# Gates and gated products of two mixers computed with tokens on the partitions, with the gated sum transposed

## The chip, the cores and the metric

The kernel runs on one core of one Trainium2 chip. The metric is the device time of one launch in microseconds (us); the comparison is by medians of several runs. The engines are named PE (TensorE, matrix multiplications), DVE (VectorE), ACT (ScalarE), POOL (GpSimd) and SP (SyncE, which here only starts the weight transfers). PSUM is the memory into which PE adds up its results; DVE and ACT read it.

## The reference

The input x has 256 tokens of 1024 features, in float32. Two blocks follow one another. In outline (the attention branches themselves are cut):

```python
# first block
h    = rmsnorm(x, norm_mix)
proj = h @ w_in                      # queries, keys, values, ..., and 2 x 1024 gate columns
o_a  = dsa_mixer(...)                # 256 x 512
o_b  = nsa_mixer(...)                # 256 x 512
mix  = (sigmoid(gate_a) * (o_a @ w_branch_a)
        + sigmoid(gate_b) * (o_b @ w_branch_b))
x    = x + mix @ w_out
x    = x + square(relu(rmsnorm(x) @ w_mlp_in)) @ w_mlp_out
# second block: swiglu, hybrid mixer, swiglu; the mixer ends with
merged = (sigmoid(g_a) * (att @ w_att_branch)       # att: 256 x 512
          + sigmoid(g_m) * (ml @ w_mlstm_branch))   # ml: 256 x 1024
y      = merged @ w_out
```

The change is in the four sigmoid gates, the four products that they multiply, and the two sums `mix` and `merged`.

## The kernel before

**Precision by splitting.** Every float32 operand of a large product is split in two parts, `hi` (rounded) and `lo` (the rest), and a product is three matmuls: hi·hi, hi·lo and lo·hi. Weights come in units of 512 KB (2 tiles of 128 rows by 512 columns) on SP's queue, five units ahead (`stream_dma`); `stream_split` makes `hi` on ACT (L262) and `lo` on DVE (L263), two units ahead.

**Two forms of a product.** One chunk is 512 columns of a weight matrix with K rows.
- `gemm_feat` (L335 to L360) keeps 128 columns of the weights in PE (the stationary operand) and moves all 256 tokens past them (L349, L351, L352). For K = 1024 a chunk is 8 x 4 x 3 = 96 matmuls of 256 columns. The result has features on the partitions.
- `gemm_tok` (L285 to L330) keeps 128 tokens in PE and moves 512 weight columns past them (L305, L306, L307). The same chunk is 8 x 2 x 3 = 48 matmuls of 512 columns. The result has tokens on the partitions, in two tiles, `t` = 0 and 1. With `tail=n` the last n units go to token tile 0 first and then to tile 1, so that tile 0 is complete earlier.

Each of the two forms fills two PSUM buffers of 128 x 512 per chunk; the pool `pacc` has three. A function `done` empties each as it is complete.

**Pending jobs.** Other work (attention steps, transposes) waits in a list, `pending`. Both forms take `rate` jobs from it after each tile of K, from tile `delay` on, so this work lies between the matmuls of a chunk. What is written between them is then moved again: the program's scheduler sets the order on PE, ACT and DVE by its own estimate of times; POOL and SP follow the order as written.

**From tokens to features.** A product needs its left operand with features on the partitions. `split_T` makes such an operand from a token tile by jobs; for each tile of K, `split_one` runs two PE transposes (L399), one ACT copy that makes `hi` (L406) and one DVE subtraction that makes `lo` (L407). Where the data has features on the partitions already, `split_sb` does it without PE (L1124 on ACT, L1125 on DVE).

**First mixer.** Chunks 5 to 8 of `W_IN1` are the gates (L1008). Each half chunk is multiplied on DVE by the inverse norm of its tokens (`bc2`, L1002), passes through Tanh on ACT (L1003) and is scaled on POOL (L1004). Between these matmuls the attention steps are taken from the list: logits (L869), row maximum and bias on DVE (L882), exp on ACT (L887), transposes (L896), copies to SBUF on DVE (L898), products with the values (L909). Then come `W_BRB` and `W_BRA` (K = 512, two chunks each): `bdone` (L1025) multiplies by the gate, `adone` (L1032, L1033) does the same, adds and calls `split_sb`. `W_OUT1` follows with `gemm_tok`.

**Second mixer.** Chunks 18 to 21 of `W_IN2` are the gates `gta` and `gtm` (L1542, L1543), among the chunks of a convolution (`cdone`) that keeps features on the partitions. The output gate `gto` of chunks 16 and 17 is done by tokens already: one Tanh that reads PSUM with a scale per token (L1493). `W_ATT` (K = 512) and `W_MLB` (K = 1024) are the gated products, and the sum `mb` goes through `split_sb` to `W_OUT2`, which is in `down_post`.

The three functions of the diff are the first mixer, `down_post` and the second mixer.

Of the kernel before, what the change touches and what calls it, by code (L numbers as in the profile page):

```python
# [9 lines left out]
F32 = mybir.dt.float32  # L10
# [3 lines left out]
AF = mybir.ActivationFunctionType  # L14
ALU = mybir.AluOpType
# [6 lines left out]
D = 1024  # L22
# [187 lines left out]
class Prog:  # L210
# [352 lines left out]
    def block1_mix(self, x0, x):  # L563
        tc, nc, ap, g = self.tc, self.nc, self.ap, self.g
        with ExitStack() as es, ExitStack() as rs_:
# [431 lines left out]
            gate = cp.tile([128, 16, 256], F32, name="gate")  # L997

            def gdone(c):
                def f(i, ps):  # L1000
                    gsl = gate[:, 4 * c + 2 * i:4 * c + 2 * i + 2, :]
                    nc.vector.tensor_tensor(gsl, ps, bc2, op=ALU.mult)  # L1002
                    nc.scalar.activation(gsl, gsl, AF.Tanh, scale=0.5)  # L1003
                    nc.gpsimd.tensor_scalar(gsl, gsl, 0.5, 0.5, op0=ALU.mult, op1=ALU.add)  # L1004
                return f
            for c in range(4):
                self.gemm_feat(W_IN1, 5 + c, *xT, gdone(c))
                if c == 0:  # L1008
                    bias_rows(0)
# [7 lines left out]
            mixt = self.xp.tile([128, 8, 256], F32, tag="x", name="mixt")  # L1017
            mTp = rpool("mixT", 1)
            l3p = rpool("late", 2)
            mT = [mTp.tile([128, 8, 256], F32R, name="mT%d" % i) for i in range(2)]  # L1020

            def bdone(c):
                def f(i, ps):
                    k = 4 * c + 2 * i
                    nc.vector.tensor_tensor(mixt[:, k:k + 2, :], ps, gate[:, 8 + k:10 + k, :], op=ALU.mult)  # L1025
                return f

            def adone(c):
                def f(i, ps):
                    k = 4 * c + 2 * i  # L1030
                    ma = l3p.tile([128, 2, 256], F32, tag="ma", name="ma")
                    nc.vector.tensor_tensor(ma, ps, gate[:, k:k + 2, :], op=ALU.mult)  # L1032
                    nc.vector.tensor_tensor(ma, ma, mixt[:, k:k + 2, :], op=ALU.add)  # L1033
                    self.split_sb(ma, mT, k)
                return f
            self.later(*ja)
            for c in range(2):
                self.gemm_feat(W_BRB, c, *obT, bdone(c))
                self.gemm_feat(W_BRA, c, *oaT, adone(c))
# [3 lines left out]
            def odone(c):  # L1043
                def f(t, ps):
                    cs = slice(c * 512, c * 512 + 512)
                    nc.vector.tensor_tensor(x[:, t, cs], ps, x[:, t, cs], op=ALU.add)
                return f
            for c in range(2):
                self.gemm_tok(W_OUT1, c, *mT, odone(c), delay=1, rate=2)
                self.later(*jx[4 * c:4 * c + 4])  # L1050
# [100 lines left out]
    def down_post(self, W, hT, gi, x, mul, name, rs=None, gcol=None):  # L1151
# [61 lines left out]
        self.gemm_tok(W, 0, *hT, done0, delay=1, rate=2)  # L1213
# [34 lines left out]
    def mixer2(self, x):  # L1248
        tc, nc, ap, g = self.tc, self.nc, self.ap, self.g
        xT, js = self.nextT  # L1250
        with ExitStack() as es, ExitStack() as rs_:
# [283 lines left out]
            gta = g2p.tile([128, 8, 256], F32, name="gta")  # L1535
            gtm = g2p.tile([128, 8, 256], F32, name="gtm")
            bc2 = rsB.unsqueeze(1).to_broadcast([128, 2, 256])

            def gfeat(dst, c):
                def f(i, ps):  # L1540
                    gsl = dst[:, 4 * c + 2 * i:4 * c + 2 * i + 2, :]
                    nc.vector.tensor_tensor(gsl, ps, bc2, op=ALU.mult)  # L1542
                    nc.scalar.activation(gsl, gsl, AF.Tanh, scale=0.5)  # L1543
                    nc.gpsimd.tensor_scalar(gsl, gsl, 0.5, 0.5, op0=ALU.mult, op1=ALU.add)
                return f
# [5 lines left out]
            self.gemm_feat(W_IN2, 18, *xT, gfeat(gta, 0))  # L1551
            self.gemm_feat(W_IN2, 12, *xT, cdone(2))
            self.gemm_feat(W_IN2, 19, *xT, gfeat(gta, 1))
# [49 lines left out]
            self.gemm_feat(W_IN2, 20, *xT, gfeat(gtm, 0))  # L1603
            self.later(job(mpv, 2), job(mpv, 3), job(mnorm, 2))
            self.gemm_feat(W_IN2, 21, *xT, gfeat(gtm, 1))
            self.flush()

            mgt = self.xp.tile([128, 8, 256], F32, tag="x", name="mgt")

            def adone(c):  # L1610
                def f(i, ps):
                    fs = slice(4 * c + 2 * i, 4 * c + 2 * i + 2)
                    nc.vector.tensor_tensor(mgt[:, fs, :], ps, gta[:, fs, :], op=ALU.mult)
                return f

            def mdone(c):
                def f(i, ps):
                    k = 4 * c + 2 * i
                    fs = slice(k, k + 2)
                    mb = m4p.tile([128, 2, 256], F32, tag="mb", name="mb")  # L1620
                    nc.vector.tensor_tensor(mb, ps, gtm[:, fs, :], op=ALU.mult)
                    nc.vector.tensor_tensor(mb, mb, mgt[:, fs, :], op=ALU.add)
                    self.split_sb(mb, mT, k)
# [30 lines left out]
```

## Time and profile before

| | us |
|---|---|
| median of 3 runs (lowest, highest) | 1115.84 (1114.71, 1116.51) |
| the profiled execution, its own time | 1113.66 |
| its span in the profile | 1111.9 |
| PE busy (6852 matmuls) | 1094.0 |
| PE weight loads busy | 978.1 |
| DVE busy | 760.2 |
| ACT busy | 574.0 |
| POOL busy | 95.9 |

The span is the time from the first to the last instruction in the profile; 1.8 us of the execution's own time lie around it. The granted clock of TensorE was its higher level all through the span. A matmul's record goes from its start to the modelled end of its results, so the records of neighbouring matmuls overlap, and the distance between the starts of two is what one of them takes of PE's time. The products of the change lie between 75 and 186 us (first mixer) and between 749 and 891 us (second mixer).

### The profile page before, as it was taken

The page shows a single profiled execution, that of the slowest core. Times are in us where ns is not written, and L with a number is a line of the kernel's source. Part 1 is how long each engine was busy: PE and PEld are TensorE (multiplying, and loading weights), DVE is VectorE, ACT ScalarE, POOL GpSimd, SP SyncE. Part 2 cuts the span into 40 slices and gives each one's busy share as a digit, 9 for nine tenths or more (in the row PEclk, how much of TensorE's full clock was granted, in tenths as well). Part 3 has the DMA queues.
Part 4 walks back from the last instruction along what each step waited for, and adds up shares of the span by engine and source line. Part 5 has one row for each costly group of instructions (what it writes and reads, how often), then busy time and mean ns, then how long its engine had stood idle before and what let it go on. Part 6 is the DMA issues. An engine that isn't in the chain of part 4 may idle for free.

```text
span 1111.9 us, 17700 instructions
## 1 busy us (share of the span) xinstructions
PE 1094.0 (98%) x6852; PEld 978.1 (88%) x6852; DVE 760.2 (68%) x1230; ACT 574.0 (52%) x858; POOL 95.9 (9%) x143
## 2 busy tenths in 40 slices
PE   8999999999999999999999999999999999999997
PEld 8898899888888788888879999889999978888886
DVE  6777768587745487776457675557788776777643
ACT  6334554465545365555545336455466456655552
POOL 0422410000001000000010100001313000000000
PEclk9999999999999999999999999999999999999999
DMA  8864235565555556555556646434545465555552
GB/s 298 238 231 114 77 111 182 182 190 190 190 193 191 192 180 191 190 190 190 190 159 202 206 137 209 150 120 162 173 152 172 159 199 165 182 185 189 189 177 89
DMA packets 56036, 196.91 MB, mean 177 GB/s; under 512 B 6844, under 2 KB 7116, under 8 KB 55696
## 3 DMA queue, kind: packets, MB, share of 16 engines
q1 hardware_dynamic: 52704, 186.44, 51.6%
q0 software_dynamic: 2960, 9.21, 3.4%
q8 instruction: 54, 0.88, 0.3%
q14 instruction: 30, 0.25, 0.1%
q10 hardware_dynamic: 288, 0.14, 0.1%
HBM read 192.84 MB, written 1.44 MB: 175 GB/s over the span
## 4 chain that ended last, share of the span: by engine, by line
PE 93%; DMA 3%; DVE 2%; ACT 1%; issue 0%; POOL 0%; DVEq 0%; SPq 0%; ACTq 0%; POOLq 0%
PE acc L368 20%; PE acc L369 10%; PE acc L305 10%; PE acc L306 10%; PE acc L307 10%; PE acc L349 8%; PE acc L351 8%; PE acc L352 8%; PE o L909 1%; PE sm L869 1%; DMA w1k<-in_cmp_w_k 1%; PE tr L896 1%; PE o L1455 1%; PE sm L1425 1%; PE tr L399 1%; DMA w1v<-in_cmp_w_v 1%
## 5 line engine op out<-in xcount | busy, mean ns | idle before, releaser
L263 DVE TENSOR_TENSOR lo<-raw,hi 128x1024 fp32r<-128x1024 f32 (+2 forms) x356 | 431.7, 1215 | 255.0 <-ACT hi L262 253.0
L262 ACT ACTIVATE hi<-raw 128x1024 fp32r<-128x1024 f32 (+2 forms) x356 | 371.2, 1044 | 422.2 <-PE acc L351 128.9
L368 PE MATMUL acc<-xs,hi 128*128 128x512 f32 x960 | 338.5, 398 | 1.3 <-DVE sum L374 1.0
L369 PE MATMUL acc<-xs,lo 128*128 128x256 f32 x960 | 267.6, 280 | 0.0
L368 PEld LDWEIGHTS acc<-xs,hi 128*128 128x128 f32 x960 | 180.7, 189 | 43.8 <-DVE sum L374 1.4
L349 PE MATMUL acc<-xs,hi 128*128 128x256 f32 (+1 forms) x696 | 198.1, 287 | 0.3 <-ACT hi L262 0.3
L351 PE MATMUL acc<-xs,hi 128*128 128x256 f32 (+1 forms) x696 | 197.7, 285 | 0.0
L352 PE MATMUL acc<-xs,lo 128*128 128x256 f32 (+1 forms) x696 | 196.9, 285 | 0.1
L369 PEld LDWEIGHTS acc<-xs,lo 128*128 128x128 f32 x960 | 181.6, 189 | 0.5
L349 PEld LDWEIGHTS acc<-xs,hi 128*128 128x128 f32 (+1 forms) x696 | 132.4, 191 | 3.1 <-issue 1.9
L351 PEld LDWEIGHTS acc<-xs,hi 128*128 128x128 f32 (+1 forms) x696 | 132.9, 191 | 1.9 <-issue 1.3
L352 PEld LDWEIGHTS acc<-xs,lo 128*128 128x128 f32 (+1 forms) x696 | 132.4, 191 | 1.5 <-issue 1.0
L305 PE MATMUL acc<-hi,hT 128*128 128x512 f32 x304 | 117.9, 390 | 1.0 <-DVE x L1087 1.0
L306 PE MATMUL acc<-lo,hT 128*128 128x512 f32 x304 | 118.5, 390 | 0.0
L307 PE MATMUL acc<-hi,hT 128*128 128x512 f32 x304 | 118.0, 389 | 0.0
L305 PEld LDWEIGHTS acc<-hi,hT 128*128 128x128 f32 x304 | 57.0, 188 | 13.3 <-DVE x L1087 1.5
L307 PEld LDWEIGHTS acc<-hi,hT 128*128 128x128 f32 x304 | 57.1, 188 | 12.0
L306 PEld LDWEIGHTS acc<-lo,hT 128*128 128x128 f32 x304 | 57.1, 188 | 11.6
L305 PE MATMUL acc<-hi,xs 128*128 128x386 f32 (+1 forms) x128 | 47.7, 375 | 1.6 <-DVE f L1178 1.5
L306 PE MATMUL acc<-lo,xs 128*128 128x386 f32 (+1 forms) x128 | 47.9, 375 | 0.0
L307 PE MATMUL acc<-hi,xs 128*128 128x386 f32 (+1 forms) x128 | 46.7, 370 | 0.0
L374 DVE TENSOR_TENSOR sum<-acc,sum 128x512 f32<-128x512 f32 x60 | 41.0, 684 | 0.0
(430 smaller groups left out, 1333.0 us busy)
## 6 DMA issues: line engine op xcount, KB each, us to landing
raw<-in_w_in SPq DMA_DIRECT2D x100, 512.0 KB, 3.7
raw<-in_ffn_w_gate SPq DMA_DIRECT2D x44, 512.0 KB, 4.2
raw<-in_ffn_w_up SPq DMA_DIRECT2D x44, 512.0 KB, 4.3
raw<-in_ffn_w_down SPq DMA_DIRECT2D x44, 512.0 KB, 4.2
raw<-in_w_mlp_in SPq DMA_DIRECT2D x32, 512.0 KB, 3.3
raw<-in_w_mlp_out SPq DMA_DIRECT2D x32, 512.0 KB, 3.3
raw<-in_w_out SPq DMA_DIRECT2D x16, 512.0 KB, 3.6
raw<-in_w_in SPq DMA_DIRECT2D x16, 386.0 KB, 3.1
```

What stands on the lines that cost most here:

```text
L262: nc.scalar.activation(hi[:, :n * w], raw[:, :n * w], AF.Copy)
L263: nc.vector.tensor_tensor(lo[:, :n * w], raw[:, :n * w], hi[:, :n * w], op=ALU.subtract)
L305: nc.tensor.matmul(ps[t][:, :w], xh[:, k, sl], hi, start=(k == 0), stop=False)
L306: nc.tensor.matmul(ps[t][:, :w], xh[:, k, sl], lo, start=False, stop=False)
L307: self.last_mm = nc.tensor.matmul(ps[t][:, :w], xl[:, k, sl], hi, start=False, stop=last)
L349: nc.tensor.matmul(o, hi[:, fs], xh[:, k, :], start=(k == 0 and f % 2 == 0), stop=False, skip_group_check=True)
L351: nc.tensor.matmul(o, hi[:, fs], xl[:, k, :], start=False, stop=False, skip_group_check=True)
L352: nc.tensor.matmul(o, lo[:, fs], xh[:, k, :], start=False, stop=last, skip_group_check=True)
L368: nc.tensor.matmul(ps[:, f, :, :], hi[:, fs], x.both[:, k, :, :], start=(k == 0), stop=False)
L369: nc.tensor.matmul(ps[:, f, 0, :], lo[:, fs], x.hi[:, k, :], start=False, stop=last)
L374: nc.vector.tensor_tensor(s, ps[:, :, 0, :], s, op=ALU.add)
L399: nc.tensor.transpose(ps[:, i * 128:i * 128 + 128], src(t, k), self.ident)
```

## The change

In both mixers the gate chunks and the gated products go from `gemm_feat` to `gemm_tok`. The gate tiles and the sums have tokens on the partitions. The multiplication by the inverse norm is left out as an instruction of its own: it becomes the per-token scale of a Tanh that reads PSUM (in the first mixer a small DVE instruction makes the scale `rh0`). The sum is written back to `mixt` and `mgt`, and eight `split_T` jobs in each mixer (`jm`, sixteen PE transposes) take the place of four calls of `split_sb`. The second chunk of `W_BRA` and of `W_MLB` completes token tile 0 first (`tail`), and the products after them start to take jobs one tile of K later (`delay=2`).

```diff
-            gate = cp.tile([128, 16, 256], F32, name="gate")
+            gate = cp.tile([128, 2, 2 * D], F32, name="gate")
+            rh0 = self.small(2, "r0h")
+            nc.vector.tensor_scalar(rh0, r0, 0.5, None, op0=ALU.mult)
 
             def gdone(c):
-                def f(i, ps):
-                    gsl = gate[:, 4 * c + 2 * i:4 * c + 2 * i + 2, :]
-                    nc.vector.tensor_tensor(gsl, ps, bc2, op=ALU.mult)
-                    nc.scalar.activation(gsl, gsl, AF.Tanh, scale=0.5)
+                def f(t, ps):
+                    gsl = gate[:, t, c * 512:c * 512 + 512]
+                    nc.scalar.activation(gsl, ps, AF.Tanh, scale=rh0[:, t:t + 1])
                     nc.gpsimd.tensor_scalar(gsl, gsl, 0.5, 0.5, op0=ALU.mult, op1=ALU.add)
                 return f
             for c in range(4):
-                self.gemm_feat(W_IN1, 5 + c, *xT, gdone(c))
+                self.gemm_tok(W_IN1, 5 + c, *xT, gdone(c))
...
-            mixt = self.xp.tile([128, 8, 256], F32, tag="x", name="mixt")
+            mixt = self.xp.tile([128, 2, D], F32, tag="x", name="mixt")
...
+            jm = self.split_T(lambda t, k: mixt[:, t, k * 128:k * 128 + 128], range(8), [0, 1], *mT)
...
             def adone(c):
-                def f(i, ps):
-                    k = 4 * c + 2 * i
-                    ma = l3p.tile([128, 2, 256], F32, tag="ma", name="ma")
-                    nc.vector.tensor_tensor(ma, ps, gate[:, k:k + 2, :], op=ALU.mult)
-                    nc.vector.tensor_tensor(ma, ma, mixt[:, k:k + 2, :], op=ALU.add)
-                    self.split_sb(ma, mT, k)
+                def f(t, ps):
+                    cs = slice(c * 512, c * 512 + 512)
+                    ma = l3p.tile([128, 512], F32, tag="ma", name="ma")
+                    nc.vector.tensor_tensor(ma, ps, gate[:, t, cs], op=ALU.mult)
+                    nc.vector.tensor_tensor(mixt[:, t, cs], ma, mixt[:, t, cs], op=ALU.add)
                 return f
             self.later(*ja)
             for c in range(2):
-                self.gemm_feat(W_BRB, c, *obT, bdone(c))
-                self.gemm_feat(W_BRA, c, *oaT, adone(c))
+                self.gemm_tok(W_BRB, c, *obT, bdone(c))
+                self.gemm_tok(W_BRA, c, *oaT, adone(c), tail=c)
+                self.later(*jm[4 * c:4 * c + 4])
...
             for c in range(2):
-                self.gemm_tok(W_OUT1, c, *mT, odone(c), delay=1, rate=2)
+                self.gemm_tok(W_OUT1, c, *mT, odone(c), delay=1 if c else 2, rate=2)
                 self.later(*jx[4 * c:4 * c + 4])
...
-        self.gemm_tok(W, 0, *hT, done0, delay=1, rate=2)
+        self.gemm_tok(W, 0, *hT, done0, delay=2 if self.pop else 1, rate=2)
...
             self.gemm_feat(W_IN2, 10, *xT, cdone(0))
-            self.gemm_feat(W_IN2, 18, *xT, gfeat(gta, 0))
+            self.gemm_tok(W_IN2, 18, *xT, gdone(gta, 0))
             self.gemm_feat(W_IN2, 12, *xT, cdone(2))
-            self.gemm_feat(W_IN2, 19, *xT, gfeat(gta, 1))
+            self.gemm_tok(W_IN2, 19, *xT, gdone(gta, 1))
...
-            self.gemm_feat(W_ATT, 0, *attT, adone(0))
-            self.gemm_feat(W_ATT, 1, *attT, adone(1), rate=2)
+            self.gemm_tok(W_ATT, 0, *attT, adone(0))
+            self.gemm_tok(W_ATT, 1, *attT, adone(1), rate=2)
...
+            jm = self.split_T(lambda t, k: mgt[:, t, k * 128:k * 128 + 128], range(8), [0, 1], *mT)
             for c in range(2):
-                self.gemm_feat(W_MLB, c, *mlT, mdone(c), delay=1)
+                self.gemm_tok(W_MLB, c, *mlT, mdone(c), delay=1, tail=2 * c)
+                self.later(*jm[4 * c:4 * c + 4])
```

The left-out parts do for `bdone`, the second mixer's `adone`, `mdone` and the chunks 20 and 21 what the parts shown do.

The end of the first mixer's attention on PE, before. `L869` are logits, `L909` products with the values, `L896` transposes of the softmax; `xs` and `hi` or `lo` in `acc<-xs,hi` are the tokens and the weights of a gate chunk.

```order
L349 MATMUL acc<-xs,hi 128x256
L869 MATMUL sm<-ka,qa 128x128 x6
L909 MATMUL o<-tms,PT 128x64 x8
L869 MATMUL sm<-ka,qa 128x128
L896 MATMUL tr<-ident,L 128x128 x8
L351 MATMUL acc<-xs,hi 128x256
L352 MATMUL acc<-xs,lo 128x256
L349 MATMUL acc<-xs,hi 128x256
```

These are the last logits; 121 gate matmuls follow them, among the rest of the attention, up to the first matmul of `W_BRB`. Now the same place after the change; the last gate matmul stands five rows above the first row, and `ob` and `obT` are the attention's output and its transposed form.

```order
L896 MATMUL tr<-ident,L 128x128 x5
L869 MATMUL sm<-ka,qa 128x128 x8
L909 MATMUL o<-tms,PT 128x64 x4
L896 MATMUL tr<-ident,L 128x128 x4
L909 MATMUL o<-tms,PT 128x64 x4
L896 MATMUL tr<-ident,L 128x128 x4
L399 MATMUL tr<-ident,ob_1079 128x128
L399 MATMUL tr<-ident,ob_1080 128x128
L909 MATMUL o<-tms,PT 128x64 x4
L305 MATMUL acc<-hi,obT_1076 128x512
L306 MATMUL acc<-lo,obT_1076 128x512
```

The gate matmuls have moved ahead of the last logits, and between the last steps of the attention there are a few matmuls of `W_BRB`, of which the first two rows are shown.

The start of `W_OUT1` on PE, before: `oaT` is the left operand of `W_BRA`, `mT` that of `W_OUT1`.

```order
L351 MATMUL acc<-oaT_1075,hi 128x256
L352 MATMUL acc<-oaT_1074,lo 128x256
L305 MATMUL acc<-hi,mT_2156 128x512
L306 MATMUL acc<-lo,mT_2156 128x512
L307 MATMUL acc<-hi,mT_2157 128x512
```

`W_OUT1` ran through its tiles of K without a break. After the change, from the last matmuls of its first four tiles of K on:

```order
L305 MATMUL acc<-hi,mT_1958 128x512
L306 MATMUL acc<-lo,mT_1958 128x512
L307 MATMUL acc<-hi,mT_1959 128x512 x2
L399 MATMUL sm<-ident,mixt 128x128
L399 MATMUL tr<-ident,mixt 128x128
L399 MATMUL sm<-ident,mixt 128x128
L399 MATMUL tr<-ident,mixt 128x128
L305 MATMUL acc<-hi,mT_1958 128x512
L399 MATMUL sm<-ident,mixt 128x128
L399 MATMUL tr<-ident,mixt 128x128
```

Of the 16 new transposes of the first mixer eight stand here, behind the first 24 matmuls of `W_OUT1`. The single `L305` between them belongs to the second chunk of `W_OUT1`.

## Rows read from the trace of the kernel before

**Rows 1.** The page: busy time of each engine, and the chain's shares by engine.

```profile
PE 1094.0 (98%) x6852; PEld 978.1 (88%) x6852; DVE 760.2 (68%) x1230; ACT 574.0 (52%) x858; POOL 95.9 (9%) x143
...
PE 93%; DMA 3%; DVE 2%; ACT 1%; issue 0%; POOL 0%; DVEq 0%; SPq 0%; ACTq 0%; POOLq 0%
```

**Rows 2.** Windows: stretch, length, busy PE, PEld, DVE, ACT, POOL (instructions), clock, DMA, GB/s.

```profile
75.00:150.00 75.00, 75.00 (x612) 67.83 (x611) 55.06 (x179) 40.01 (x126) 20.77 (x24) 1.00 0.35 99
...
625.00:650.00 25.00, 25.00 (x211) 25.00 (x210) 17.01 (x19) 8.47 (x8) 2.51 (x6) 1.00 0.58 171
830.00:854.00 24.00, 23.95 (x190) 23.36 (x188) 21.71 (x34) 12.52 (x18) 9.28 (x10) 1.00 0.51 159
1050.00:1075.00 25.00, 25.00 (x112) 20.71 (x111) 12.05 (x11) 9.98 (x10) 0.00 (x0) 1.00 0.60 193
```

**Rows 3.** Costliest groups, one of each form: instructions, busy us, mean ns.

```profile
L349 PE MATMUL acc<-xs,hi 128*128 128x256 f32 (+1 forms) x696 | 198.1, 287 | 0.3 <-ACT hi L262 0.3
...
L305 PE MATMUL acc<-hi,hT 128*128 128x512 f32 x304 | 117.9, 390 | 1.0 <-DVE x L1087 1.0
```

**Rows 4.** Timeline of PE, `gemm_feat`: start, duration; first and last of 43 matmuls.

```profile
624.90 0.28 PE L349 MATMUL acc<-xs,hi 128*128 128x256 f32 x1
...
629.94 0.28 PE L349 MATMUL acc<-xs,hi 128*128 128x256 f32 x1
```

**Rows 5.** Timeline of PE, `gemm_tok`: the first and the last of 46 matmuls.

```profile
1055.78 0.39 PE L307 MATMUL acc<-hi,hT 128*128 128x512 f32 x1
...
1065.98 0.39 PE L307 MATMUL acc<-hi,hT 128*128 128x512 f32 x1
```

**Rows 6.** Timeline of PE, four transposes between matmuls of `gemm_tok`.

```profile
202.02 0.40 PE L307 MATMUL acc<-hi,mT 128*128 128x512 f32 x1
202.25 0.38 PE L399 MATMUL sm<-ident,x 128*128 128x128 f32 x2
202.47 0.38 PE L399 MATMUL tr<-ident,x 128*128 128x128 f32 x2
202.61 0.49 PE L305 MATMUL acc<-hi,mT 128*128 128x512 f32 x1
202.93 0.39 PE L306 MATMUL acc<-lo,mT 128*128 128x512 f32 x1
```

**Rows 7.** Timeline of PE, two logits matmuls between gate matmuls.

```profile
88.70 0.28 PE L351 MATMUL acc<-xs,hi 128*128 128x256 f32 x1
88.91 0.70 PE L869 MATMUL sm<-kv,qb 64*128 64x256 f32 x2
89.53 0.39 PE L352 MATMUL acc<-xs,lo 128*128 128x256 f32 x1
89.76 0.28 PE L349 MATMUL acc<-xs,hi 128*128 128x256 f32 x1
```

**Rows 8.** Groups by line and form: instructions, busy us, mean ns, idle before them.

```profile
L263 DVE TENSOR_TENSOR lo<-raw,hi 128x1024 fp32r<-128x1024 f32 x332 | 409.6, 1236 | 243.0 <-ACT hi L262 241.1 <-PE sm L399 0.6
...
L898 DVE COPY PT<-tr 128x512 f32<-128x512 f32 x18 | 12.0, 684 | 5.0 <-PE tr L896 5.0
...
L887 ACT ACTIVATE L<-L,nn 128x128 f32<-128x128 f32 x24 | 9.3, 389 | 5.1 <-DVE nn L885 5.0
L887 ACT ACTIVATION_READ_ACCUMULATOR L<-L,nn 128x1 f32 x48 | 9.0, 187 | 0.0
...
L1002 DVE TENSOR_TENSOR gate<-acc,rsB 128x512 f32<-128x512 f32 x8 | 5.5, 689 | 2.1 <-PE acc L352 2.0
...
L399 PE MATMUL tr<-ident,x 128*128 128x128 f32 x28 | 5.2, 274 | 0.5 <-DVE x L1046 0.5
...
L1493 ACT ACTIVATE gto<-acc,m_rh 128x512 f32<-128x512 f32 x4 | 2.7, 689 | 2.6 <-PE acc L307 2.6
...
L407 DVE TENSOR_TENSOR obT<-tr,obT 128x256 fp32r<-128x256 f32 x4 | 1.7, 420 | 0.0
...
L406 ACT ACTIVATE obT<-tr 128x256 fp32r<-128x256 f32 x4 | 1.5, 378 | 3.5 <-PE tr L399 3.4
```

More of the change, by code (lines that the diff above doesn't have):

```diff
@@ L1020, in block1_mix, with f @@
             mT = [mTp.tile([128, 8, 256], F32R, name="mT%d" % i) for i in range(2)]
+            jm = self.split_T(lambda t, k: mixt[:, t, k * 128:k * 128 + 128], range(8), [0, 1], *mT)
             def bdone(c):
-                def f(i, ps):
-                    k = 4 * c + 2 * i
-                    nc.vector.tensor_tensor(mixt[:, k:k + 2, :], ps, gate[:, 8 + k:10 + k, :], op=ALU.mult)
+                def f(t, ps):
+                    cs = slice(c * 512, c * 512 + 512)
+                    nc.vector.tensor_tensor(mixt[:, t, cs], ps, gate[:, t, D + c * 512:D + c * 512 + 512],
+                                            op=ALU.mult)
                 return f
             def adone(c):
-                def f(i, ps):
-                    k = 4 * c + 2 * i
-                    ma = l3p.tile([128, 2, 256], F32, tag="ma", name="ma")
-                    nc.vector.tensor_tensor(ma, ps, gate[:, k:k + 2, :], op=ALU.mult)
-                    nc.vector.tensor_tensor(ma, ma, mixt[:, k:k + 2, :], op=ALU.add)
-                    self.split_sb(ma, mT, k)
+                def f(t, ps):
+                    cs = slice(c * 512, c * 512 + 512)
+                    ma = l3p.tile([128, 512], F32, tag="ma", name="ma")
+                    nc.vector.tensor_tensor(ma, ps, gate[:, t, cs], op=ALU.mult)
+                    nc.vector.tensor_tensor(mixt[:, t, cs], ma, mixt[:, t, cs], op=ALU.add)
                 return f
@@ L1534, in mixer2 @@
             wp = rpool2("mw", 2)
[L1535 to L1545, printed above, removed]
+            gta = g2p.tile([128, 2, D], F32, name="gta")
+            gtm = g2p.tile([128, 2, D], F32, name="gtm")
             hm = hp.tile([128, 2, 4, 256], F32, name="hm")
@@ L1602, in mixer2, with f @@
             self.later(*jh[0:4], job(mst, 2), job(mst, 3))
-            self.gemm_feat(W_IN2, 20, *xT, gfeat(gtm, 0))
+            self.gemm_tok(W_IN2, 20, *xT, gdone(gtm, 0))
             self.later(job(mpv, 2), job(mpv, 3), job(mnorm, 2))
-            self.gemm_feat(W_IN2, 21, *xT, gfeat(gtm, 1))
+            self.gemm_tok(W_IN2, 21, *xT, gdone(gtm, 1))
             self.flush()
-            mgt = self.xp.tile([128, 8, 256], F32, tag="x", name="mgt")
+            mgt = self.xp.tile([128, 2, D], F32, tag="x", name="mgt")
             def adone(c):
-                def f(i, ps):
-                    fs = slice(4 * c + 2 * i, 4 * c + 2 * i + 2)
-                    nc.vector.tensor_tensor(mgt[:, fs, :], ps, gta[:, fs, :], op=ALU.mult)
+                def f(t, ps):
+                    cs = slice(c * 512, c * 512 + 512)
+                    nc.vector.tensor_tensor(mgt[:, t, cs], ps, gta[:, t, cs], op=ALU.mult)
                 return f
             def mdone(c):
[L1617 to L1623, printed above, removed]
+                def f(t, ps):
+                    cs = slice(c * 512, c * 512 + 512)
+                    mb = m4p.tile([128, 512], F32, tag="mb", name="mb")
+                    nc.vector.tensor_tensor(mb, ps, gtm[:, t, cs], op=ALU.mult)
+                    nc.vector.tensor_tensor(mgt[:, t, cs], mb, mgt[:, t, cs], op=ALU.add)
                 return f
             self.later(None, *jh[4:8])
-            self.gemm_feat(W_ATT, 0, *attT, adone(0))
-            self.gemm_feat(W_ATT, 1, *attT, adone(1), rate=2)
+            self.gemm_tok(W_ATT, 0, *attT, adone(0))
+            self.gemm_tok(W_ATT, 1, *attT, adone(1), rate=2)
             self.flush()
```

## The prediction

> **What bounds the kernel now.** I read the page first. PE is busy 1094.0 of 1111.9 us and makes up 93% of the chain that ended last [rows 1], so only PE's time, or a wait that PE is given, moves the end. Then I asked for PE's waits from 75 to 209 us and from 590 to 912 us, where the change lies: the view has no entry in either. The windows say the same, with other engines well below full: in the first mixer's gates DVE is busy 55.06 and ACT 40.01 of 75 us; the tightest place is the second mixer's end, with DVE at 21.71 of 24 us [rows 2]. So work taken from DVE or ACT gives nothing by itself, and the question is what the new instructions take of PE.
>
> A busy PE can't be priced from the mean of a record, because records overlap. So I looked at the starts, in stretches without other work. In `gemm_feat` 43 matmuls start from 624.90 to 629.94, 5.04 / 42 = 120.0 ns apart [rows 4]; in `gemm_tok` 46 start from 1055.78 to 1065.98, 10.20 / 45 = 226.7 ns apart [rows 5]. Counting the records of a window is a rougher way, since those that cross its edges count whole: 25 us with 211 gives 118.5 ns, with 112 gives 223 ns [rows 2]. Weight loads fill the first kind of window wholly, 25.00 of 25 us, and the second to 20.71 [rows 2]: a 256-column matmul hardly outlasts the load that runs beside it.
>
> **The change part by part.**
>
> *Products.* Moved are ten chunks with K = 1024 (eight of gates, two of `W_MLB`) and six with K = 512: 10 x 96 + 6 x 48 = 1248 matmuls of 256 columns go, 10 x 48 + 6 x 24 = 624 of 512 columns come. In pairs: 624 x (2 x 120.0 - 226.7) = 624 x 13.3 ns = -8.3 us, all on the path. With the windows' counts instead (118.5 and 223) it is 624 x 14 = -8.7. On the other side, if each tile of K lost as much as the stretch of [rows 6] shows at its end (0.32 us from `L305` to `L306`, less 0.227), in a tenth of the 104 tiles of K, 1 us would go: -7.3. These are the bounds.
>
> *Transposes.* Sixteen per mixer, 32 in all, come to PE. In the timeline four of them lie between matmuls of `gemm_tok`: from 202.02 to 202.93 are two of those matmuls and four transposes, 0.91 - 2 x 0.227 = 0.456 us, or 114 ns each [rows 6]. 32 x 114 ns = +3.65 us. Their mean record is 274 ns [rows 8], which is latency.
>
> The Trainium skill, "TensorE: Matmul & The Clock Gate" (Part 4: PE-mode transpose), speaks against this: it gives about 275 ns for a transpose within a kernel. The trace has the same figure as the length of a record, but not as what PE loses to it. By the page the sum below would be 5.2 us higher.
>
> *Split entries.* A pair of logits matmuls among gate matmuls took 89.76 - 88.70 - 2 x 0.12 = 0.82 us [rows 7], against 0.24 for two matmuls of 256 columns at full spacing: about 0.58 us is paid for breaking the stream. In the new order the `L869` of 64 rows stand in 19 pieces instead of 17. 2 x 0.58 = +1.2, from 0 (a piece may end up beside another of its kind) to 1.2; I take 1.0.
>
> *End of the first mixer's attention.* Before, 121 gate matmuls follow the last logits, some 14.5 us of work that hides the softmax. Now the gate chunks run out first, and behind the last eight logits PE has, up to the softmax's last transposes, 28 small matmuls or transposes at 0.114 and six matmuls of `W_BRB` at 0.227: 4.6 us. The softmax of those eight takes ACT 8 x (0.389 + 0.187) = 4.6 us [rows 8], starting some 0.7 us later, when the first logits have been reduced: about 0.7 us of wait. A product with the values that waits for a copy (0.684) behind other work on DVE adds 0.5. I take +1.2. Below it the bound is 0 (the exps keep up). Above, two copies that stand behind one `lo` subtraction each, 2 x (0.684 + 1.236) = 3.8 us [rows 8], so 4. Behind the waiting matmul on PE stands the rest of the program, so such a wait is lost in full.
>
> *Gates out of PSUM.* DVE loses 16 multiplications of 0.689, 11 us; ACT's Tanh reads PSUM and lasts 0.689 as `gto`'s does [rows 8]. This hides under PE. But the buffer is now freed by ACT, and in the second mixer's order two of the four gate chunks' Tanhs stand behind the Tanh of a convolution half, which waits for DVE. With three buffers the first tile has about six matmuls, 1.4 us, before it is missed. `gto`, done so already, left no entry among PE's waits. I take 0, with 0 to 2 us (a `lo` and a gate instruction late on DVE, 1.236 + 0.684).
>
> *Sum and transposed sum.* The products with the gates have as many instructions as before on DVE. The four `split_sb` of each mixer become eight pairs of 0.378 on ACT and 0.420 on DVE [rows 8], 6.4 us per mixer on the two together, beside the matmuls of `W_OUT1` and `W_OUT2`. What is late next is `mT`'s second half. In `W_OUT1` the tile of K that needs it comes behind 24 matmuls, 5.4 us, and a few of the second chunk: 0. In `W_OUT2` the eight transposes stand in a row, and the first matmul behind them needs ACT and DVE, 0.8 us, of which six other transposes cover 0.7, if no `lo` of 1.236 stands before: +0.3, from 0 to 1.5. The extra `r0h` on DVE is small, beside PE's gate matmuls: 0. The weight units on SP's queue and the order of the feed-forward blocks stay as they are.
>
> *Sum.* -8.3 + 3.65 + 1.0 + 1.2 + 0 + 0.3 = -2.15, say -2.1 us. The profiled execution took 1113.66 us (its span of 1111.9 and 1.8 around it), so it would become 1111.6. That execution is 2.2 us below the median of the runs, 1115.84; carried over to the median the forecast is 1113.7 us. With all the low ends it is -8.7 + 3.65 = -5.0; the high ends together give -7.3 + 3.65 + 1.2 + 4 + 2 + 1.5 = +5.0.
>
> **The rivals.** A measurement of this kernel can tell about 0.2%, 2.2 us, from no change.
>
> A. *Nothing waits.* Only the products and transposes count, with one broken stream at most: -8.3 + 3.65 + 0.6 = -4.1, 1111.7 us. For it: no wait of PE in either stretch before, and DVE gets 11 us lighter. Against: the order has no gate matmul left among the last steps of the attention.
>
> B. *The gain is eaten.* The PSUM buffer of a gate waits for ACT in two of the second mixer's four chunks, about 1 us each: -2.1 + 2.0 = -0.1, 1115.7 us. For it: DVE at 90% there. Against: `gto`'s evictions, and a lighter DVE.
>
> C. *Slower, by the uncovered softmax.* If the exps of the last two groups do not run ahead of PE, it waits for both: twice 8 x 0.576 = 4.6 us and two copies of 0.684, less the 4.6 us of work: 6.0 us in the place of 1.2. The sum is then -2.1 + 4.8 = +2.7, 1118.5 us. It decides from a wait of 5.5 us on, where the whole is 2.2 us slower. For it: the rows of the new order. Against: ACT was busy 40 of 75 us, so it should keep ahead.
>
> D. *The transposes cost their records.* 32 x (0.274 - 0.114) = 5.1 us more: +3.0, 1118.8 us. Against it stand the starts [rows 6].
>
> E. *The mean records count.* Then a chunk falls from 96 x 287 to 48 x 390 ns [rows 3], 8.8 us, and 13 such chunks give -115 us. The starts exclude it, since 96 x 287 ns would not fit into a chunk's time of 11.5 us.
>
> **How the numbers follow.** The forecast has a chance of 0.50 with a range of its own from 1112.2 to 1115.3; A 0.20, B 0.14, C 0.12, D 0.03, E 0.01. A lies beyond the bound of 2.2 us on the fast side, and so does a little under half of the forecast's share (the sum is 0.1 us short of it): 0.20 + 0.24 + 0.01 = 0.45 faster. C, D and a little of B are slower, 0.16. The rest, 0.39, is no difference. The range takes in A and C with a margin of 1 us, and stops short of the sums of all ends: 1110.5 to 1119.5.
>
> **What would show it.** In the profile of the changed kernel starts of gate matmuls 0.227 us apart with no idle time, and some 590 PE instructions fewer. `W_BRB` begins about where it did (four gate chunks, 4 x 48 x 13.3 ns = 2.6 us gained, broken streams and a wait lost). PE's waits should have entries of about a microsecond together at `L896` and `L909` before it. Four transposes between matmuls should again take 0.46 us. I am wrong if PE waits over 3 us at the attention's end (C), if a gate chunk's first matmul waits for ACT (B), or if the starts of 512-column matmuls of the gates, with attention work among them, are wider than 227 ns, for then the first term is too large.

## The result and the profile after

The changed kernel takes 1121.46 us (median of 4 runs, 1120.00 to 1121.82) against 1116.07 us before in the same measurement. The ratio is 1.0051, with an interval of 1.0034 to 1.0068: 5.4 us slower, where the forecast was 2.1 us faster with a range up to 1119.5. The span of the profiled execution grew by 7.5 us, from 1111.9 to 1119.4.

Waits explain less than half of it. PE's idle time in the span grew from 17.9 to 21.0 us; the other 4.4 us are busy time, with 592 matmuls fewer than in [rows 1]:

```profile
PE 1098.4 (98%) x6260; PEld 947.2 (85%) x6260; DVE 752.3 (67%) x1223; ACT 573.7 (51%) x866; POOL 93.7 (8%) x143
```

Between 70 and 215 us the view of PE's waits has two entries, both at the end of `W_OUT1` (columns: who waited for whom, us in all, times, longest):

```profile
PE tr L399 <- DVE x L1049: 1.1, 1, 1.1
PE acc L368 <- DVE x L1049: 0.3, 1, 0.3
```

The granted clock was not at its higher level all through the span, as was said of the kernel before. In both kernels it was at the lower one in the first microseconds and the last, and around the start of the second swiglu. There PE had been waiting for DVE, 1.8 us in the kernel before. In that kernel the stretch was from 915.35 to 922.18 us, in the changed one from 922.30 to 929.12. The row of the kernel before (stretch, length, busy PE, PEld, DVE, ACT, POOL, granted clock, DMA, GB/s):

```profile
915.35:922.18 6.83, 6.15 (x22) 5.04 (x22) 4.78 (x11) 3.51 (x8) 0.00 (x0) 0.50 0.37 116
```

So I cut the timeline of PE by stages, from the first matmul of each to the first of the next:

| stage | before, us | changed, us | difference |
|---|---|---|---|
| start, `W_IN1`, `W_BRB`, `W_BRA` | 185.9 | 187.7 | +1.8 |
| `W_OUT1` | 24.06 | 25.69 | +1.6 |
| feed-forward in, first block | 89.54 | 89.63 | +0.1 |
| feed-forward out, first block (`hT`) | 89.42 | 91.70 | +2.3 |
| gate and up, first swiglu | 124.88 | 126.82 | +1.9 |
| down, first swiglu (`hT`) | 61.91 | 63.64 | +1.7 |
| `W_IN2` to the output gates | 173.68 | 173.70 | 0.0 |
| convolution, gates, `W_ATT`, `W_MLB` | 141.31 | 137.95 | -3.4 |
| `W_OUT2` | 26.52 | 28.94 | +2.4 |
| gate and up, second swiglu | 127.85 | 125.12 | -2.7 |
| down, second swiglu (`hT`) | 66.81 | 68.49 | +1.7 |

Of the first row's +1.8 us, 1.3 were there ahead of everything that was changed: the last matmul that reads `w1v`, an attention weight, began at 69.82 us instead of 68.51.

The three stages marked `hT` are 5.7 us longer, and the change touches none of them: same instructions, same order. What changed is the distance between two matmuls there. The timeline of the changed kernel, the first and last of 46 such matmuls (start, duration in us):

```profile
1059.79 0.40 PE L307 MATMUL acc<-hi,hT 128*128 128x512 f32 x1
...
1070.29 0.40 PE L307 MATMUL acc<-hi,hT 128*128 128x512 f32 x1
```

10.50 / 45 = 233.3 ns, where it was 226.7 [rows 5], at a granted clock of 1.00 in both. A window that lies in the same stage as that of [rows 2] has 109 matmuls in 25 us where it had 112:

```profile
1055.00:1080.00 25.00, 25.00 (x109) 20.13 (x108) 11.63 (x10) 9.90 (x11) 0.00 (x0) 1.00 0.57 188
```

912 matmuls of this kind times 6.6 ns are 6.0 us. What can differ in code that is the same is where its data lie. In the built program of before, `hT` of the first block starts at byte 118784 of each partition, a multiple of 4096; in the changed one at 118816. The new small tile `r0h` of two elements takes a slot of 32 bytes, and the attention tiles, `gate`, `obT`, `oaT`, `attT` and all `hT`, which are placed behind it, move by 32. The tokens `xs`, the weights `hi` and `lo`, `mT` and `mlT` stay where they were. Matmuls that hold one of these in PE and move 512 columns keep their distance, 227 to 229 ns.

### The profile page after: what moved, and what is told of

The parts are those of the page before. It is cut to its first block, busy times and chain, and to the rows that moved or that the text cites. A ratio compares the mean times of both kernels' runs of the same rounds, so it can differ in the third digit from the quotient of the medians.

```text
span 1119.4 us, 16519 instructions
## 1 busy us (share of the span) xinstructions
PE 1098.4 (98%) x6260; PEld 947.2 (85%) x6260; DVE 752.3 (67%) x1223; ACT 573.7 (51%) x866; POOL 93.7 (8%) x143
## 4 chain that ended last, share of the span: by engine, by line
PE 92%; DMA 3%; DVE 2%; ACT 1%; issue 1%; POOL 0%; DVEq 0%; ACTq 0%; POOLq 0%
PE acc L368 20%; PE acc L306 14%; PE acc L305 14%; PE acc L307 14%; PE acc L369 10%; PE acc L349 4%; PE acc L351 4%; PE acc L352 4%; PE sm L869 1%; DMA w1k<-in_cmp_w_k 1%; PE o L909 1%; PE tr L399 1%; PE o L1458 1%; PE sm L1428 1%; DMA w1v<-in_cmp_w_v 1%; PE tr L896 1%
## 5 line engine op out<-in xcount | busy, mean ns | idle before, releaser
L349 PE MATMUL acc<-xs,hi 128*128 128x256 f32 (+1 forms) x440 | 124.7, 286 | 0.3 <-ACT hi L262 0.3
L351 PE MATMUL acc<-xs,hi 128*128 128x256 f32 (+1 forms) x440 | 124.3, 283 | 0.0
L352 PE MATMUL acc<-xs,lo 128*128 128x256 f32 (+1 forms) x440 | 123.9, 284 | 0.0
L305 PE MATMUL acc<-hi,hT 128*128 128x512 f32 x304 | 119.7, 396 | 1.0 <-DVE x L1090 1.0
L307 PE MATMUL acc<-hi,hT 128*128 128x512 f32 x304 | 119.9, 396 | 0.0
L305 PE MATMUL acc<-hi,xs 128*128 128x512 f32 (+1 forms) x256 | 97.9, 386 | 1.6 <-DVE f L1181 1.5
L306 PE MATMUL acc<-lo,xs 128*128 128x512 f32 (+1 forms) x256 | 98.7, 386 | 0.0
L307 PE MATMUL acc<-hi,xs 128*128 128x512 f32 (+1 forms) x256 | 97.1, 382 | 0.0
L349 PEld LDWEIGHTS acc<-xs,hi 128*128 128x128 f32 (+1 forms) x440 | 83.6, 191 | 1.8 <-issue 0.9
L351 PEld LDWEIGHTS acc<-xs,hi 128*128 128x128 f32 (+1 forms) x440 | 84.0, 191 | 0.7 <-issue 0.3
L352 PEld LDWEIGHTS acc<-xs,lo 128*128 128x128 f32 (+1 forms) x440 | 83.7, 191 | 0.5 <-issue 0.3
L305 PEld LDWEIGHTS acc<-hi,hT 128*128 128x128 f32 x304 | 57.1, 188 | 15.2 <-DVE x L1090 1.4
L305 PEld LDWEIGHTS acc<-hi,xs 128*128 128x128 f32 x256 | 48.1, 188 | 9.8 <-ACT xs L402 1.9
```

The lines of the kernel that those rows point to most:

```text
L305: nc.tensor.matmul(ps[t][:, :w], xh[:, k, sl], hi, start=(k == 0), stop=False)
L306: nc.tensor.matmul(ps[t][:, :w], xh[:, k, sl], lo, start=False, stop=False)
L307: self.last_mm = nc.tensor.matmul(ps[t][:, :w], xl[:, k, sl], hi, start=False, stop=last)
L349: nc.tensor.matmul(o, hi[:, fs], xh[:, k, :], start=(k == 0 and f % 2 == 0), stop=False, skip_group_check=True)
L351: nc.tensor.matmul(o, hi[:, fs], xl[:, k, :], start=False, stop=False, skip_group_check=True)
L352: nc.tensor.matmul(o, lo[:, fs], xh[:, k, :], start=False, stop=last, skip_group_check=True)
```

## The experiments

Each was timed against the kernel before on the same chip. "Shift" is the number of bytes by which the tiles behind the small ones are moved.

**Shift 64 (x1_align).** The change, with a wider `r0h`.

```diff
-            rh0 = self.small(2, "r0h")
+            rh0 = self.small(16, "r0h")[:, 0:2]
```

> The change, with the small tile r0h made 64 bytes wide per partition instead of 8, so that the SBUF tiles placed behind it lie 64 bytes later than before and not 32. Theory S (shift): the 5.4 us come from the places of tiles. In the changed kernel the matmuls of 512 columns that keep hT in PE start 233.3 ns apart instead of 226.7; 912 of them and 144 with obT, oaT or attT make 1056 x 6.6 ns = 7.0 us. Then this kernel has 226.7 ns there again and takes 1121.5 - 7.0 = 1114.5 us, 1.6 us less than before (ratio 0.9986). Theory O (order): the loss is made in the mixers, by the new order and by waits at the attention's end; then the places do nothing and it stays at 1121.5 (ratio 1.005).

Measured: 1122.51 us, ratio 1.0062 (1.0044 to 1.0081). That is what theory O said, but the trace shows why: 64 bytes are no better than 32. The first and last of 49 matmuls, 11.20 / 48 = 233.3 ns:

```profile
1059.71 0.39 PE L307 MATMUL acc<-hi,hT 128*128 128x512 f32 x1
...
1070.91 0.39 PE L307 MATMUL acc<-hi,hT 128*128 128x512 f32 x1
```

**Shift 32 alone (x2_shift).** The kernel before with the two lines of `r0h`; nothing reads it.

```diff
             gate = cp.tile([128, 16, 256], F32, name="gate")
+            rh0 = self.small(2, "r0h")
+            nc.vector.tensor_scalar(rh0, r0, 0.5, None, op0=ALU.mult)
```

> The kernel before, with only the small tile r0h of 8 bytes and the DVE instruction that fills it; nothing reads it. Theory S: the same tiles move by 32 bytes, 912 matmuls with hT take 6.6 ns more each: +6.0 us, 1122.1 (ratio 1.005); the 256-column matmuls, in which obT, oaT and attT move, should show whether a moved operand off its old place costs too. Theory O: one DVE instruction of under 0.2 us beside PE's work, 1116.1 (ratio 1.000).

Measured: 1119.95 us, ratio 1.0040 (1.0023 to 1.0056). The stages with `hT` took 2.26, 1.74 and 1.69 us more, as in the changed kernel, and 45 matmuls lie 10.26 / 44 = 233.2 ns apart:

```profile
1059.64 0.40 PE L306 MATMUL acc<-lo,hT 128*128 128x512 f32 x1
...
1069.90 0.40 PE L305 MATMUL acc<-hi,hT 128*128 128x512 f32 x1
```

Most of the loss is there without any of the change's matmuls.

**One mixer at a time (x3_mix1, x4_mix2).** The parts of the change in the first mixer alone, with `r0h` of 64 bytes; and those in the second mixer and `down_post` alone, where no small tile is added.

```diff
-                self.gemm_feat(W_IN1, 5 + c, *xT, gdone(c))
+                self.gemm_tok(W_IN1, 5 + c, *xT, gdone(c))
...
-            self.gemm_feat(W_IN2, 18, *xT, gfeat(gta, 0))
+            self.gemm_tok(W_IN2, 18, *xT, gdone(gta, 0))
```

The first two lines and what belongs to them are in x3_mix1 only, the last two in x4_mix2 only.

> The change in the first mixer alone, with r0h made 64 bytes wide; the second mixer as before. By the terms of the forecast: 288 pairs x 13.3 ns = -3.8, 16 transposes +1.8, broken streams +1.0, the attention's end +1.2: +0.2 us, 1116.3 (ratio 1.000). If the attention's end without gate matmuls costs what rival C said, 6 us: +5, 1121 (1.0045).

> The change in the second mixer and in W_OUT2 alone; the first mixer as before, no r0h. By the terms of the forecast: 336 pairs x 13.3 ns = -4.5, 16 transposes +1.8, W_OUT2 +0.3: -2.4 us, 1113.7 (ratio 0.998). If gates wait for ACT to empty PSUM (rival B): -0.4, 1115.7.

Measured: the first mixer alone 1124.51 us, ratio 1.0086 (1.0060 to 1.0112); the second alone 1115.10 us, ratio 0.9989 (0.9975 to 1.0002). The first seemed to bear out rival C, and does not: of its loss 5.7 us again lie in the three stages with `hT`, which were shifted by 64. In x4_mix2, with no shift, they are as before to 0.1 us. Of the rest of the first one's loss 1.7 us lie ahead of `W_OUT1`, too little for C, and 1.6 in it. The gain of x4_mix2, 1.2 us, can't tell the two that were expected apart; its trace can. No wait of PE for a gate's PSUM is in it, and `W_OUT2` is 2.2 us longer, where 0.9 for its transposes and 0.3 for a wait were counted.

**No shift (x5_noshift).** `rh0` in room that the slot of `r0` has left.

```diff
-            r0 = self.small(2, "r0")
+            r0w = self.small(4, "r0")
+            r0 = r0w[:, 0:2]
...
-            rh0 = self.small(2, "r0h")
+            rh0 = r0w[:, 2:4]
```

> The change, with the scale rh0 kept in unused room of an existing small tile (r0 made 4 elements wide within its 32 bytes), so that no tile lies elsewhere than in the kernel before. With 64 bytes of shift the matmuls with hT stayed at 233 ns, so 64 bytes are no safe step; here the shift is 0. Theory S: 226.7 ns again in all 912 matmuls with hT and about 227 in the 144 with obT, oaT and attT, 6.7 us less than the changed kernel in the profile: 7.5 - 6.7 = 0.8 us more than before, ratio 1.001. Theory O: the shift is beside the point, hT stays slow for another reason: ratio 1.005.

Measured: 1116.58 us, ratio 1.0005 (0.9994 to 1.0016), as theory S said. The order of every instruction is that of the changed kernel. 46 matmuls lie 10.20 / 45 = 226.7 ns apart:

```profile
1055.67 0.39 PE L305 MATMUL acc<-hi,hT 128*128 128x512 f32 x1
...
1065.87 0.39 PE L305 MATMUL acc<-hi,hT 128*128 128x512 f32 x1
```

**Shift 128 and 256 (x6_shift128, x12_shift256).** The kernel before with an unread small tile.

```diff
+            rh0 = self.small(32, "r0h")[:, 0:2]
+            nc.vector.tensor_scalar(rh0, r0, 0.5, None, op0=ALU.mult)
```

The other has 64 in the place of 32.

> The kernel before, with an unread small tile of 128 bytes, so that everything behind it moves by 128 bytes. If 128 bytes keep the place of hT as good as it was, the 912 matmuls stay at 226.7 ns and the ratio is 1.000. If the step has to be larger, they take 233 ns: +6.0 us, ratio 1.005.

> The kernel before, with an unread small tile of 256 bytes, so that everything behind it moves by 256 bytes. The matmuls with attT and obT, which lay at a multiple of 256 bytes, took 227 ns in the kernels without shift; so if only the step of 256 matters, the 912 matmuls with hT stay at 226.7 ns: ratio 1.000. If it is the old place itself that is good (a multiple of 4096 for hT), they take 233 ns: +6.0 us, ratio 1.005.

Measured: with 128 bytes 1122.21 us, ratio 1.0057 (1.0038 to 1.0075), 45 matmuls 10.24 / 44 = 232.7 ns apart; with 256 bytes 1117.01 us, ratio 1.0002 (0.9993 to 1.0011), 46 matmuls 226.7 ns apart. First the rows of 128, then of 256:

```profile
1059.70 0.40 PE L307 MATMUL acc<-hi,hT 128*128 128x512 f32 x1
...
1069.94 0.40 PE L306 MATMUL acc<-lo,hT 128*128 128x512 f32 x1
```

```profile
1059.70 0.39 PE L305 MATMUL acc<-hi,hT 128*128 128x512 f32 x1
...
1069.90 0.39 PE L305 MATMUL acc<-hi,hT 128*128 128x512 f32 x1
```

So here the matmuls keep their pace where the tile that PE holds starts at a multiple of 256 bytes, and 32, 64 and 128 bytes past one are about equally bad. Other offsets were not run.

**Without token tile 0 first (x9_notail).** No shift, no `tail`, and `delay=1` in both output products.

```diff
-                self.gemm_tok(W_BRA, c, *oaT, adone(c), tail=c)
+                self.gemm_tok(W_BRA, c, *oaT, adone(c))
...
-                self.gemm_tok(W_OUT1, c, *mT, odone(c), delay=1 if c else 2, rate=2)
+                self.gemm_tok(W_OUT1, c, *mT, odone(c), delay=1, rate=2)
```

> The change without shift, and without the part that completes token tile 0 first: no tail in the second chunks of W_BRA and W_MLB, delay=1 in W_OUT1 and W_OUT2. If that part hides the wait for the last gated sum, two splits and their transposes are late by about 0.7 (product) + 0.7 (sum) us per mixer, up to 2.8 us in all: ratio 1.002 to 1.0035. If other work covers it: as the change without shift, 1.001.

Measured: 1116.08 us, ratio 0.9999 (0.9988 to 1.0009). That part of the change makes no measurable difference: other matmuls cover the last gated sum.

**Gates held back (x8_pace, x11_pace5, x13_lag2, x14_lag3).** All without shift. A gate tile of K may not be issued before certain logits, so that gate matmuls are left for the attention's end. The core of the edit, as in x14_lag3 (`anchors` holds the last logits matmul of each group):

```diff
-                for t in range(2):
-                    mm(kt, t)
+                with ExitStack() as es:
+                    if pace and len(self.anchors) > 3:
+                        es.enter_context(self.tc.issue_after(self.anchors[-4].ins))
+                    for t in range(2):
+                        mm(kt, t)
...
-                self.gemm_tok(W_IN1, 5 + c, *xT, gdone(c))
+                self.gemm_tok(W_IN1, 5 + c, *xT, gdone(c), rate=1 if c < 2 else 2, pace=True)
```

x8_pace waits for the latest logits; x11_pace5 does so only from the sixth tile of the first gate chunk on; x13_lag2 has a lag of two groups and `rate=1`. The other three also take two jobs after each tile of K from the third gate chunk on (`rate`), and that was not run apart from the holding back.

> The change without shift, and each tile of K of a gate chunk in the first mixer issued no earlier than the logits written ahead of it, so that 78 gate matmuls stand behind the last logits instead of none. In the changed kernel the first mixer up to W_OUT1 took 1.6 us more than before where the forecast had 1.7 less, 0.6 of the gap by the shift. Theory T (attention's end): most of the other 2.7 us is lost where the softmax has no gate matmul beside it; then this is 2 to 2.7 us faster than the change without shift, ratio about 0.9985 against before. Theory P (pieces): the loss is in the switches of PE between gates and attention; then the two are the same within 0.7 us.

> The paced change without shift, in which the first five tiles of K of the first gate chunk are not paced, so that 38 gate matmuls stand ahead of the first logits instead of 26. In the paced run PE waited 0.9 us for ACT there, and then ran at a granted clock of 0.57 from 78 to 86 us. Theory T with this explanation: gates and attention up to W_BRB lose neither the wait nor the slow clock, 3 to 4 us less than the paced run, ratio about 0.995 against before. If the slow clock was only in that one profile, or if the pieces cost as much: the same as the paced run, 0.998.

> The change without shift, in which a gate tile of K is issued no earlier than the logits written two groups ahead of it: 50 gate matmuls before the first logits (67 without pacing, 26 and 38 in the two paced runs, whose granted clock fell to 0.5 there) and 47 behind the last. Theory T (attention's end): without the fall of the clock the gain of the paced order shows in full; the stretch from the gates to W_OUT1 takes 164 to 167 us instead of 170.0, ratio 0.9945 to 0.998. Theory P (pieces and switches): 170 us, ratio 1.0005. If the clock falls again: 168 us and 0.998.

> The same with a lag of three groups and two jobs for each tile of K from the third gate chunk on: 67 gate matmuls before the first logits, as in the change without shift, and 39 behind the last. The start of the attention is then as in the change without shift, whose clock stayed high, and only its end differs. Theory T: 164 to 167 us to W_OUT1, ratio 0.9945 to 0.998. Theory P: 170 us, 1.0005.

Measured, against before: x8_pace 1113.90 us, ratio 0.9977 (0.9965 to 0.9989); x11_pace5 1115.09, 0.9991 (0.9979 to 1.0002), so the 0.995 expected of theory T was wrong; x13_lag2 1113.49, 0.9981 (0.9969 to 0.9994); x14_lag3 1110.77, 0.9952 (0.9934 to 0.9970). The last is faster than both kernels: 4.8 us under before, some 10 under the change.

Why x11_pace5 gained nothing more is in its windows (stretch, length, busy PE, PEld, DVE, ACT, POOL, then the granted clock):

```profile
72.00:82.00 10.00, 9.05 (x66) 7.29 (x64) 5.41 (x15) 4.54 (x14) 0.00 (x0) 0.99 0.36 123
82.00:90.00 8.00, 7.82 (x22) 4.64 (x21) 5.27 (x28) 4.02 (x16) 0.00 (x0) 0.50 0.12 46
90.00:100.00 10.00, 10.00 (x67) 8.48 (x66) 7.64 (x26) 5.90 (x18) 3.46 (x7) 0.89 0.26 73
```

PE stood idle for 0.95 us before 82 us, and then ran at the lower of the clock's two levels for some 10 us. That was not in this profile alone: the mean granted clock of its twelve runs was 0.990 to 0.994, that of the kernel before beside it 0.994 to 0.998. An idle PE alone does not tell when: x13_lag2 waited 1.2 us for DVE at the same place, and its granted clock stayed at 1.00 in its profile. In x14_lag3, whose start of the attention is that of the change without shift, it does not fall there, and about twice as many matmuls, though not the same ones, pass in the same 8 us:

```profile
82.00:90.00 8.00, 8.00 (x43) 6.04 (x43) 5.41 (x14) 3.95 (x6) 5.76 (x10) 1.00 0.76 200
```

From the start to `W_OUT1` x14_lag3 took 180.5 us, the change without shift 187.1; of the 6.6 us 0.9 lie ahead of the attention. Part of the rest is the softmax at the end: the transposes took 10.1 us of records instead of 11.1. The larger part is the logits, as groups by form show (instructions, busy us, mean ns), first of the changed kernel, then of x14_lag3:

```profile
L896 PE MATMUL tr<-ident,L 128*128 128x128 f32 x72 | 11.1, 281 | 0.2
L869 PE MATMUL sm<-kv,qb 64*128 64x256 f32 x32 | 6.6, 412 | 0.0
L869 PE MATMUL sm<-ka,qa 64*128 64x256 f32 x16 | 3.9, 422 | 0.0
L869 PE MATMUL sm<-kv,qb 64*128 64x128 f32 x32 | 3.8, 304 | 0.0
L869 PE MATMUL sm<-ka,qa 64*128 64x128 f32 x16 | 1.2, 285 | 0.0
```

```profile
L904 PE MATMUL tr<-ident,L 128*128 128x128 f32 x72 | 10.1, 275 | 0.0
L875 PE MATMUL sm<-kv,qb 64*128 64x256 f32 x32 | 5.9, 409 | 0.0
L875 PE MATMUL sm<-kv,qb 64*128 64x128 f32 x32 | 2.3, 285 | 0.0
L875 PE MATMUL sm<-ka,qa 64*128 64x256 f32 x16 | 2.3, 402 | 0.0
L875 PE MATMUL sm<-ka,qa 64*128 64x128 f32 x16 | 1.2, 285 | 0.0
```

The same logits (96 records) take 15.5 us in 19 pieces and 11.7 us in 11. By distances between starts, which don't overlap, the logits are 3.5 us shorter, the transposes 0.7 and the products with the values 0.5. Theory T was right in its figures: from the gates to `W_OUT1` it took 164.0 us, where 164 to 167 were expected, x13_lag2 took 166.2, and theory P, which expected no gain, was wrong in its own. But by the rows the larger gain, some 3.5 us, is not at the attention's end; it goes with logits that stand in fewer pieces, which is P's cause. Some 1 us is T's. The two, and `rate`, were not run apart, so the cause of the gain is argued from these rows and not shown.

## Why the prediction was wrong, step by step

*The extra `r0h`.* This is the step that failed: "The extra `r0h` on DVE is small, beside PE's gate matmuls: 0." The instruction costs nothing (x12_shift256 has it too); its tile does, by moving others. It cost 5.7 us in the three stages with `hT`, and 0.5 us in the 1056 - 912 = 144 matmuls with `obT`, `oaT` and `attT`: `W_BRB` with `W_BRA` took 23.2 us instead of 22.9 without shift, `W_ATT` 15.1 instead of 14.9. Without it the change is 0.6 us slower than before (interval -0.7 to +1.8); with it, 5.4. Those medians lie 4.8 us apart and not 6.2, and one stage goes the other way: gate and up of the second swiglu is faster with the shift (last section). The sentence on the feed-forward blocks, whose order stays as it is, was true and led past the point. No rival had a place outside the mixers.

*Products, -8.3.* Right in the second mixer: convolution, gates, `W_ATT` and `W_MLB` are 3.56 us shorter in the change without shift, with 8 transposes in them, 0.9 us; so the products gave 4.5 by this difference, and the forecast's share is 336 x 13.3 ns = 4.5. In the first mixer gates and branch products gave 2.9 of 3.8 us there, by the distances from each of their matmuls to the next start: 72.3 us before, 69.4 without shift.

*Transposes, +3.65.* Right. In the changed kernel four of them between matmuls of `W_BRA` (start, duration):

```profile
185.67 0.40 PE L306 MATMUL acc<-lo,oaT 128*128 128x512 f32 x1
185.90 0.27 PE L399 MATMUL sm<-ident,mixt 128*128 128x128 f32 x1
186.01 0.27 PE L399 MATMUL tr<-ident,mixt 128*128 128x128 f32 x1
186.12 0.27 PE L399 MATMUL sm<-ident,mixt 128*128 128x128 f32 x1
186.23 0.27 PE L399 MATMUL tr<-ident,mixt 128*128 128x128 f32 x1
186.25 0.48 PE L307 MATMUL acc<-hi,oaT 128*128 128x512 f32 x1
186.57 0.39 PE L306 MATMUL acc<-lo,oaT 128*128 128x512 f32 x1
```

0.90 us less two matmuls of 0.23 leaves 0.44, 110 ns each, as in [rows 6]; reckoned so, the 32 new ones take 110 to 134 ns each in the six places where they lie. Rival D is out. The Trainium skill, "TensorE: Matmul & The Clock Gate" (Part 4: PE-mode transpose), gives about 275 ns for a transpose within a kernel. The trace agrees with that for the record, 0.27 us; what counted is the distance, 0.11.

*Split entries, +1.0.* Right in size: the logits took 14.8 us of records before and 15.5 in the changed kernel, +0.7. What I missed is that this was an expense to be saved, too.

*End of the attention, +1.2.* Right in size, partly by luck. PE's timeline of the changed kernel there:

```profile
153.32 1.16 PE L869 MATMUL sm<-ka,qa 64*128 64x128 f32 x16
154.61 1.10 PE L909 MATMUL o<-tms,PT 128*128 128x64 f32 x8
...
160.16 0.39 PE L896 MATMUL tr<-ident,L 128*128 128x128 f32 x2
160.31 0.72 PE L307 MATMUL acc<-hi,obT 128*128 128x512 f32 x2
160.86 1.76 PE L896 MATMUL tr<-ident,L 128*128 128x128 f32 x6
162.46 0.38 PE L399 MATMUL tr<-ident,ob 128*128 128x128 f32 x2
```

Six transposes take 1.60 us from 160.86 to 162.46, where 0.7 would do: 0.9 us for the exps. The other wait is 0.3, ahead of 154.61. Errors in the working offset each other. The forecast let the last eight exps start 0.7 us after the last logits, which began at 154.21, and gave each 0.576 us, its record and that of its sum one after the other. In the trace the first begins at 159.05, since DVE came to their row maxima only at 156.80, and they start 0.39 us apart:

```profile
159.05 0.40 ACT L887 ACTIVATE L<-L,nn 128x128 f32<-128x128 f32 x1 [0.97 <-DVE nn L885]
...
159.45 0.39 ACT L887 ACTIVATE L<-L,nn 128x128 f32<-128x128 f32 x1
```

PE had more to do meanwhile than the 4.6 us that were counted: 6.6 us lie between 154.21 and 160.86, 0.3 of them the other wait, for each product with the values stands in the trace as two records (x8 above, where the order had x4). Rival C is out; its wait would have been 6.0, and it rests on the same 0.576.

*Gates out of PSUM, 0.* Right; the waits have no entry for it, and the Tanh has the forecast length [rows 8], so rival B is out as well:

```profile
L1496 ACT ACTIVATE gta<-acc,m_rh 128x512 f32<-128x512 f32 x4 | 2.7, 690 | 2.0 <-PE acc L307 2.0
```

*`W_OUT1` 0, `W_OUT2` +0.3.* Too small. The stages are 1.6 and 2.4 us longer, of which 8 transposes each are 0.9: +0.7 and +1.5. The place was wrong too: the new transposes are covered, and what is late is the last sum of the output product itself, on DVE, which the next transposes wait for: 1.1 us at L1049 above, against 0.5 before, and 1.3 us after `W_OUT2`, against 0.3. First the two rows of before, then the changed kernel's after `W_OUT2`:

```profile
PE tr L399 <- DVE x L1046: 0.5, 1, 0.5
PE acc L399 <- DVE xn L1195: 0.3, 1, 0.3
```

```profile
PE sm L399 <- DVE xn L1198: 1.3, 1, 1.3
```

Why this sum is later than before was not tried. In x9_notail both stages are as long, so the order by token tiles is not the reason.

With the measured sizes the sum without shift is -7.4 + 3.65 + 0.7 + 1.2 + 0.7 + 1.5 = +0.35, near the 0.6 of x5_noshift. So the terms that were worked out miss by 2.5 us together, and the one put at nothing by 4.8 between the medians, or 6.2 in the stages that it slowed down. The range is not, as it says, short of the sums at both ends: 1110.5 lies below the low one, 1115.84 - 5.0 = 1110.8.

## What to carry to other kernels

Before a change is priced, compare where the tiles of the built program lie, not only its instructions: a small tile added to an early pool can move every tile placed behind it, and slow down stages that the change never touches. When a stage with the same instructions is longer and has no waits, look at the distance between the starts of its matmuls. And side work inside a stream of matmuls took less time here in fewer pieces (the logits 15.5 us of records in 19, 11.7 in 11), so it is worth trying to keep it in whole groups.

## What the runs showed of the hardware

- A matmul of 512 columns in this float32 form started 226.7 ns after the one before when the tile that PE loads (`hT`) lay at a multiple of 256 bytes, and 232.7 to 233.3 ns after it with 32, 64 or 128 bytes of offset. The records of the weight loads do not show it: their mean is 188 ns before and in the changed kernel, while that of the matmuls at L305 grew from 390 to 396. Why was not tried.
- It is otherwise for the tile that moves. In x2_shift, where `obT` and `oaT` move through matmuls of 256 columns at 32 bytes of offset, these start 113 to 120 ns apart instead of 120, and `W_BRB` with `W_BRA` was 0.6 us shorter.
- Three stages that the change doesn't touch, and whose matmuls read no shifted tile, come in different lengths: the feed-forward's first product 89.5 or 91.1 us, gate and up of the first swiglu 124.9 or 126.8, of the second 125.1 to 128.5. In the profile after this gave +1.9 and -2.7 in the table above. In the first two, kernels whose tiles all lie as before have either length, and the cause stays open; it is why kernels were compared by stages here.
- The third goes with two things that the record shows. The granted clock was at its lower level for 3.1 to 6.0 us of it, by profile. And in 100 us at a granted clock of 1.00 it has 580 or 581 matmuls in the four profiles with a shift of 32 or 64 bytes, and 567 to 570 in the ten others, those with 128 and 256 among them. Taking half of the low stretch off each length, the four are some 1.9 us shorter. Shown are before and the changed kernel. The tiles that DVE and ACT write in this stage do move, those that PE reads don't; no run was made to part the two.

```profile
940.00:1040.00 100.00, 100.00 (x567) 86.67 (x566) 73.15 (x83) 58.12 (x75) 0.00 (x0) 1.00 0.57 185
940.00:1040.00 100.00, 100.00 (x580) 88.18 (x579) 74.62 (x89) 58.12 (x75) 0.00 (x0) 1.00 0.59 194
```
